# Token loads on two queues, conditioning in 1 MB halves and four places, tokens transposed first, eight leading projections

## The chip, the cores and the metric

One core of a Trainium2 chip runs the kernel. The metric is the time of one execution on the device in microseconds, as the median of several runs; a profile is one execution recorded instruction by instruction. The engines are the tensor engine (PE, with its weight loads as PEld), the vector engine (DVE), the scalar engine (ACT), GpSimd (POOL) and SyncE (SP), which here only issues DMAs. ACT and POOL issue DMAs too. Each engine works through its own queue in order.

## What is computed

A trunk of two layers over 128 context tokens and 512 latent tokens of width 2048, all in float32. The even layer (first) mixes windowed attention (A) with a gated short convolution (B), the odd layer differential attention (C) with dense attention (D). Both project the normalized and modulated tokens with one wide matrix, and both end in an output projection:

```python
def modulation(cond, w, b):
    m = jax.nn.silu(cond) @ w + b
    ...
    return jnp.split(m, 3, axis=-1)

    for layer in range(DEPTH):
        sh_p, sc_p, gt_p = modulation(c_ctx, ada_w[layer], ada_b[layer])
        sh_s, sc_s, gt_s = modulation(c, ada_w[layer], ada_b[layer])
        hp = rms_norm(xp, norm_g[layer]) * (1.0 + sc_p) + sh_p
        hs = rms_norm(xs, norm_g[layer]) * (1.0 + sc_s) + sh_s
        ...
        xp = xp + gt_p * out_p
        xs = xs + gt_s * out_s
```

`ada_w` is 2048 x 6144 per layer, 50 MB; its first two thirds (shift and scale) of layer 0 are needed before the first projection can be finished. The even layer's `ev_w_in` is 2048 x 6656: 52 projections of 128 columns.

## The kernel before

**Layout.** Features lie on the 128 partitions, tokens along the free axis: 640 columns, in two halves of 320 (`HV`). The inner dimension 2048 is 16 k tiles of 128. Every float32 operand is split into a high and a low part (`split`: ACT makes the high part, DVE the low one), and a product is three matmuls: high x high, high x low, low x high (lines 265 to 267). One projection is 16 k tiles x 2 halves x 3 = 96 of these.

**Start.** Ten token tiles `xb` (five blocks of 128 tokens, two tiles of 512 KB each) are loaded on ACT's queue (`x_load`, line 97), small rows (`rows_a`, `rows_b`: conditioning vectors, norms, biases) on SP's and POOL's. ACT computes `th`, a tanh of the conditioning rows (line 119), DVE finishes the SiLU (120), PE transposes the rows (123, 124). `x_block` then transposes each token block: 16 transposes in four groups of four (844), each group copied out of PSUM into `xT` by DVE or, the fourth, ACT (845); ACT also takes the squares for the RMS norm (849), and POOL the power of -0.5 (853). Two PSUM tiles `T` (`psT`) alternate there. `x_rows` spreads the norm over partitions (859, 860).

**Conditioning on PE.** `ada_on_pe` computes 256 or 512 columns of shift or scale: it loads `ada_w` in pieces of 2 MB into the tiles `ada_t`, of which there are two, multiplies them with the SiLU vectors (167), copies the result on ACT (170), transposes it (173), and DVE reduces it and adds bias and gain (175, 155, 144). `ada_group(g, js)` does scale and shift for k tiles js of group g (four groups of four).

**Leading projections.** While shift and scale still arrive, `run_tiles` goes over the k tiles in *units* and does the first projections side by side, so that each weight of the conditioning unlocks work at once. `cut` splits the first and last group of four k tiles into two units, so there are six: k tiles 0-1, 2-3, 4-7, 8-11, 12-13, 14-15. In each unit `h0_maker` makes the k tile's input (882, 886, 887; `h_t` has two tiles), and then every lead gets its matmuls. Two leads are *held*, in PSUM of their own, for the whole stage; the others (`trans`) share the PSUM pair `pa`/`pb` number 0, and after each unit their result is added to a sum in SBUF: by ACT in the first unit (332), by DVE afterwards (334). Weights `raw` come in by SP (243), four places for `raw`, four each for its halves `wh` and `wl`. After a unit's first lead, `ahead` issues the conditioning of the next unit.

**Behind the leads** the remaining projections run one after another; the leads' results are taken up one by one in between (`pending`, `prep`), and after `GRACE` projections what is left is finished at once (`settle`). Per projection and quarter, 1.2 steps of a filler run (`fill0`: the remaining conditioning on DVE, line 202, 12 blocks of 16 + 1 steps).

**What sets the order.** The text is not the order in the queues: a scheduler places the instructions of each engine when the program is built. DMAs of SP and ACT take their completion semaphores from a shared set of eight in turn (DMAHW0 to DMAHW7 below), and one that reuses a semaphore waits until the DMA that had it has landed.

## Time and profile before

| what | us |
|---|---|
| median of 3 runs | 2345.85 |
| lowest, highest | 2345.31, 2351.35 |
| span of the profiled execution | 2344.7 |
| PE busy | 2285.0 (97%) |
| PEld busy | 2207.7 (94%) |
| DVE busy | 1571.3 (67%) |
| ACT busy | 929.0 (40%) |

The span is that of the profiled execution from its first to its last instruction, and what lies around it is not in it; the runs' times are of whole executions. A matmul's record in the profile is longer than its share of the time, since matmuls overlap: the distance of two starts is the pace. An engine's idle time is put down to what released it ("<-").

### The profile page before, as it was taken

The page shows a single profiled execution, that of the slowest core. Times are in us where ns is not written, and L with a number is a line of the kernel's source. Part 1 is how long each engine was busy: PE and PEld are TensorE (multiplying, and loading weights), DVE is VectorE, ACT ScalarE, POOL GpSimd, SP SyncE. Part 2 cuts the span into 40 slices and gives each one's busy share as a digit, 9 for nine tenths or more (in the row PEclk, how much of TensorE's full clock was granted, in tenths as well). Part 3 has the DMA queues.
Part 4 walks back from the last instruction along what each step waited for, and adds up shares of the span by engine and source line. Part 5 has one row for each costly group of instructions (what it writes and reads, how often), then busy time and mean ns, then how long its engine had stood idle before and what let it go on. Part 6 is the DMA issues. An engine that isn't in the chain of part 4 may idle for free.

```text
span 2344.7 us, 41429 instructions
## 1 busy us (share of the span) xinstructions
PE 2285.0 (97%) x15988; PEld 2207.7 (94%) x15988; DVE 1571.3 (67%) x3196; ACT 929.0 (40%) x1935; POOL 133.0 (6%) x181
## 2 busy tenths in 40 slices
PE   4999999999999999999999999999999999999999
PEld 2689999999999999999999999999999999999999
DVE  3457977777777663888865755854855754567576
ACT  3234442442422222544553433434434444444343
POOL 1001000000000000000010100101000000000101
PEclk9999999999999999999999999999999999999999
DMA  7986535535355542954431421512423312128642
GB/s 241 334 268 188 160 107 166 161 91 179 113 173 170 166 137 82 291 158 132 160 100 57 130 87 57 151 57 84 138 67 92 106 50 77 46 74 272 181 121 69
DMA packets 390533, 321.94 MB, mean 137 GB/s; under 512 B 18306, under 2 KB 336272, under 8 KB 389824
## 3 DMA queue, kind: packets, MB, share of 16 engines
q1 hardware_dynamic: 381536, 285.83, 40.3%
q0 software_dynamic: 7216, 28.16, 3.3%
q10 hardware_dynamic: 1584, 5.31, 0.6%
q8 instruction: 125, 2.05, 0.3%
q14 instruction: 72, 0.59, 0.1%
HBM read 290.79 MB, written 28.44 MB: 136 GB/s over the span
## 4 chain that ended last, share of the span: by engine, by line
PE 52%; DVE 2%; DMA 1%; ACT 1%; issue 1%; POOL 0%; SPq 0%; POOLq 0%; DVEq 0%; ACTq 0%
PE pa L265 5%; PE pb L266 5%; PE pb L265 5%; PE pb L267 5%; PE pa L266 5%; PE pa L267 5%; PE pq L515 4%; PE pq L517 4%; PE pq L516 4%; PE T L693 1%; PE S L705 1%; PE S L707 1%; PE S L706 1%; PE T L544 1%; DMA yin<-yd 1%; PE T L754 1%
## 5 line engine op out<-in xcount | busy, mean ns | idle before, releaser
L230 ACT ACTIVATE wh<-raw 128x512 fp32r<-128x512 f32 (+1 forms) x490 | 303.6, 620 | 806.2 <-PE pb L266 671.4
L231 DVE TENSOR_TENSOR wl<-raw,wh 128x512 fp32r<-128x512 f32 (+1 forms) x490 | 331.2, 676 | 363.2 <-ACT wh L230 337.9
L265 PE MATMUL pa<-h,wh 128*128 128x320 f32 x1760 | 560.3, 319 | 1.8 <-ACT h L230 1.5
L266 PE MATMUL pa<-h,wh 128*128 128x320 f32 x1760 | 547.0, 311 | 1.4 <-DVE h L231 1.3
L267 PE MATMUL pa<-h,wl 128*128 128x320 f32 x1760 | 545.5, 310 | 0.0
L265 PE MATMUL pb<-h,wh 128*128 128x320 f32 x1760 | 545.2, 310 | 0.0
L267 PE MATMUL pb<-h,wl 128*128 128x320 f32 x1760 | 545.1, 310 | 0.0
L266 PE MATMUL pb<-h,wh 128*128 128x320 f32 x1760 | 544.4, 309 | 0.0
L202 DVE SCALAR_TENSOR_TENSOR acc<-adaw,sT,acc 128x512 f32<-128x512 f32 (+1 forms) x600 | 357.2, 639 | 10.3 <-DMA adaw<-in_ada_w 9.6
L265 PEld LDWEIGHTS pa<-h,wh 128*128 128x128 f32 x1760 | 331.4, 188 | 23.0 <-issue 16.4
L266 PEld LDWEIGHTS pa<-h,wh 128*128 128x128 f32 x1760 | 332.0, 189 | 6.5 <-issue 2.5
L267 PEld LDWEIGHTS pa<-h,wl 128*128 128x128 f32 x1760 | 331.4, 188 | 1.2 <-issue 1.2
L267 PEld LDWEIGHTS pb<-h,wl 128*128 128x128 f32 x1760 | 330.4, 188 | 2.1 <-issue 2.1
L265 PEld LDWEIGHTS pb<-h,wh 128*128 128x128 f32 x1760 | 330.3, 188 | 1.5 <-issue 0.8
L266 PEld LDWEIGHTS pb<-h,wh 128*128 128x128 f32 x1760 | 330.4, 188 | 0.1
L679 ACT ACTIVATE p<-S,nm,rq 128x768 f32<-128x768 f32 (+3 forms) x120 | 101.2, 844 | 114.7 <-DVE nm L674 83.3
L515 PE MATMUL pq<-h,wh 128*128 128x320 f32 x352 | 109.9, 312 | 0.8 <-ACT wh L230 0.8
L516 PE MATMUL pq<-h,wh 128*128 128x320 f32 x352 | 108.7, 309 | 0.0
L517 PE MATMUL pq<-h,wl 128*128 128x320 f32 x352 | 108.4, 309 | 0.0
L672 DVE TENSOR_REDUCE nm<-S 128x1 f32<-128x768 f32 (+3 forms) x120 | 91.9, 766 | 15.9 <-PE S L707 14.8
L230 ACT ACTIVATE pth<-T 128x512 fp32r<-128x512 f32 (+1 forms) x132 | 65.9, 533 | 71.4 <-PE T L693 71.3
L516 PE MATMUL pq<-T,wh 128*128 128x320 f32 x264 | 81.4, 308 | 0.0
(301 smaller groups left out, 3382.1 us busy)
## 6 DMA issues: line engine op xcount, KB each, us to landing
raw<-in_od_w_in SPq DMA_DIRECT2D x208, 256.0 KB, 2.8
raw<-in_ev_w_in SPq DMA_DIRECT2D x196, 256.0 KB, 2.9
adaw<-in_ada_w SPq DMA_DIRECT2D x192, 256.0 KB, 2.9
ada<-in_ada_w SPq DMA_DIRECT2D x16, 2048.0 KB, 9.1
adaw<-in_ada_w SPq DMA_DIRECT2D x128, 128.0 KB, 2.2
yd<-y POOLq DMA_DIRECT2D x34, 320.0 KB, 2.7
yin<-yd SPq DMA_DIRECT2D x32, 320.0 KB, 4.7
w<-yd SPq DMA_DIRECT2D x32, 320.0 KB, 4.3
```

Of the source, the lines that this page charges most:

```text
L202: V.scalar_tensor_tensor(out=a, in0=w, scalar=sT[:, kt, c:c + 1], in1=a, op0=ALU.mult, op1=ALU.add)
L230: A.activation(hi, x, AF.Copy)
L231: V.tensor_sub(lo, x, hi)
L265: PE.matmul(ps, wh[:, i, :], hi[:, sl], start=(j == js[0] if alone else (pos == 0 and j == 0)), stop=False)
L266: PE.matmul(ps, wh[:, i, :], lo[:, sl], start=False, stop=False)
L267: PE.matmul(ps, wl[:, i, :], hi[:, sl], start=False, stop=(j == js[1] - 1 if alone else (pos == 3 and j == 3)))
L515: PE.matmul(ps, wh[:, j, :], hi, start=(h == 0 and j == 0), stop=False)
L516: PE.matmul(ps, wh[:, j, :], lo, start=False, stop=False)
L517: PE.matmul(ps, wl[:, j, :], hi, start=False, stop=(h == 1 and j == 3))
L544: PE.transpose(t[:, i * P:(i + 1) * P], src(b), ident)
L672: V.tensor_reduce(nm, s, axis=AX.X, op=ALU.max, negate=True)
L679: A.activation(p[:, 0:n], s, AF.Exp, scale=rsc, bias=nm, accum_out=l)
```

## The change

- The token tiles of blocks 0 and 1 are still loaded on ACT's queue; those of blocks 2 to 4 are now loaded on SP's queue, ahead of the conditioning. Two of the small row loads go from SP to POOL.
- The conditioning tiles become four of 1 MB in place of two of 2 MB (same total), used in turn.
- All five token blocks are transposed ahead of the first conditioning; the first shift follows right behind, and no longer as `lead_in` of the leading stage.
- Eight leads in place of six: `TRANS` has six shared projections in place of four, and the list begins with u, c, k, v, g, q, q, g (it was u, k, v, g, q, q).
- Every group of k tiles is cut, so there are eight units of two k tiles, and their conditioning blocks are 256 columns wide throughout. `keep`, which writes the transposed tokens to DRAM once a unit is done, is tied to units 6 and 7 in place of 4 and 5.

```diff
@@ -40,7 +40,7 @@
 
 P_BUFS = 4
 W_BUFS = 4
-TRANS = [0, 3, 4, 5]
+TRANS = [0, 1, 4, 5, 6, 7]
 GRACE = 3
 RAW_AHEAD = 5
 SPLIT_AHEAD = 3
@@ -94,15 +94,15 @@
         ts = []
         for g in range(2):
             ts.append(hpool.tile([P, 1024], F32, tag=f"h{15 - 2 * b - g}", name="xb"))
-            nc.scalar.dma_start(ts[g], src[:, g * 1024:(g + 1) * 1024])
+            (nc.scalar if b < 2 else nc.sync).dma_start(ts[g], src[:, g * 1024:(g + 1) * 1024])
         return ts
 
 
     nc.sync.dma_start(rows_a[0:16, :], I["c"].rearrange("b (k p) -> (b k) p", p=P))
     nc.sync.dma_start(rows_a[16:32, :], I["c_ctx"].rearrange("(k p) -> k p", p=P))
     nc.sync.dma_start(ident, I["k_ident"])
-    nc.sync.dma_start(rows_a[32:64, :], I["norm_g"].rearrange("l (k p) -> (l k) p", p=P))
-    nc.sync.dma_start(rows_a[64:112, :], I["ada_b"][0].rearrange("(k p) -> k p", p=P))
+    nc.gpsimd.dma_start(rows_a[32:64, :], I["norm_g"].rearrange("l (k p) -> (l k) p", p=P))
+    nc.gpsimd.dma_start(rows_a[64:112, :], I["ada_b"][0].rearrange("(k p) -> k p", p=P))
     xs = [x_load(b) for b in range(5)]
     rows_b = wpool.tile([P, P], F32, tag="raw", name="rows_b")
     nc.gpsimd.dma_start(rows_b[0:48, :], I["ada_b"][1].rearrange("(k p) -> k p", p=P))
@@ -111,7 +111,7 @@
     for i, n in enumerate(("a_q_norm", "c_q_norm", "d_q_norm")):
         nc.gpsimd.dma_start(rows_b[74 + i:75 + i, :], I[n])
 
-    ada_t = [pre.tile([P, 4096], F32, name=f"ada{i}") for i in range(2)]
+    ada_t = [pre.tile([P, 2048], F32, name=f"ada{i}") for i in range(4)]
     ada_sb = pre.tile([P, 512], F32, name="ada_sb")
     h_t = [pre.tile([P, NT], F32, name=f"ht{i}") for i in range(2)]
 
@@ -156,11 +156,11 @@
 
     def ada_on_pe(l, cb, h=0, n=4):
 
-        acc, m, wd = psT(), 32 // n, n * P
+        acc, m, wd = psT(), 16 // n, n * P
         for kt in range(KT):
             if kt % m == 0:
                 w = ada_t[0].rearrange("p (k n) -> p k n", k=m)
-                ada_t.reverse()
+                ada_t.append(ada_t.pop(0))
                 nc.sync.dma_start(w, I["ada_w"][l, kt * P:(kt + m) * P, cb * 512 + h * 256:cb * 512 + h * 256 + wd]
                                   .rearrange("(k p) n -> p k n", p=P))
             g = kt % 4
@@ -310,7 +310,7 @@
         lead = len(leads)
         pps = {n: (sums[n][:, 0:HALF], sums[n][:, HALF:NT]) if n in trans
                else new_pp(1 + held.index(n) if trans else n) for n in leads}
-        units = [(pos, qd, js) for pos, qd in enumerate(order) for js in (cut if cut and pos in (0, 3) else [(0, 4)])]
+        units = [(pos, qd, js) for pos, qd in enumerate(order) for js in (cut or [(0, 4)])]
         for ui, (pos, qd, js) in enumerate(units):
             raws = {n: load_raw(w_ap, jobs[n][0], qd, js) for n in leads[:W_BUFS]}
             if ui == 0 and lead_in:
@@ -868,12 +868,12 @@
             nc.sync.dma_start(band, I["k_band"])
             load_rows(sink, "a_sink")
 
-    for b in range(4):
+    for b in range(5):
         x_block(b, xs[b])
     ada_on_pe(0, 4, 0, 2)
-    x_block(4, xs[4])
     x_rows((0, 1, 2, 3))
     x_rows((4,))
+    ada_on_pe(0, 0, 0, 2)
 
     def h0_maker(k):
         x = xT[k // 4][:, k % 4, :]
@@ -892,7 +892,7 @@
 
 
     def keep(ui, n, pp):
-        g = {(4, 0): 0, (4, 4): 1, (5, 0): 2, (5, 4): 3}.get((ui, n))
+        g = {(6, 0): 0, (6, 4): 1, (7, 0): 2, (7, 4): 3}.get((ui, n))
         if g is not None:
             V.tensor_copy(xTm[g][:, 4 * NT:], pp[1][:, 0:1])
             nc.gpsimd.dma_start(x0dram[g], xTm[g])
@@ -1014,9 +1014,9 @@
         b_tiles(i)
 
     u0, c0, b0, h0, g0, g1 = jobs[4:10]
-    jobs[0:10] = [u0, jobs[0], jobs[1], g0, jobs[2], jobs[3], g1, c0, b0, h0]
+    jobs[0:10] = [u0, c0, jobs[0], jobs[1], g0, jobs[2], jobs[3], g1, b0, h0]
     run_tiles(jobs, I["ev_w_in"][0], h0_maker, fill0, FILL0, ada_group, trans=TRANS, grace=GRACE, cut=((0, 2), (2, 4)),
-              summed=keep, led=even_start, lead_in=lambda: ada_on_pe(0, 0, 0, 2))
+              summed=keep, led=even_start)
     drain(prep)
     for _ in fill0:
         pass
```

What the scheduler made of it, at three places. First ACT's queue from its beginning (`xb` are token tiles, `wh<-raw` a weight split, `sqj` the squares of a token tile). Before, from the third load on:

```order
L97 DMA xb<-in_x_sample 128x1024 [waits DMAHW0_49]
L97 DMA xb<-in_x_sample 128x1024 [waits DMAHW1_49]
L97 DMA xb<-in_x_sample 128x1024 [waits DMAHW2_49]
L97 DMA xb<-in_x_sample 128x1024 [waits DMAHW3_49]
L97 DMA xb<-in_x_sample 128x1024 [waits DMAHW5_49]
L97 DMA xb<-in_x_sample 128x1024 [waits DMAHW6_49]
L97 DMA xb<-in_x_prompt 128x1024 [waits DMAHW7_49]
L97 DMA xb<-in_x_prompt 128x1024 [waits DMAHW0_49]
L119 ACT_TABLE_LOAD
L119 ACTIVATE th<-rows_a 32x128
L849 ACTIVATE sqj,s_189<-xb 128x1024
L230 ACTIVATE wh<-raw 128x256 [waits DMAHW3_49]
```

Now:

```order
L97 DMA xb<-in_x_sample 128x1024 x3
L97 DMA xb<-in_x_sample 128x1024 [waits DMAHW1_49]
L119 ACT_TABLE_LOAD
L119 ACTIVATE th<-rows_a 32x128 [waits DMAHW2_49]
L849 ACTIVATE sqj,s_191<-xb 128x1024 [waits DMAHW0_49]
L849 ACTIVATE sqj,s_191<-xb 128x1024 [waits DMAHW5_49,Activation_49]
```

Six loads have left the queue ahead of `th`; the four weight splits that stood between the squares stand behind all token blocks now.

Second, PE's queue from its beginning, as the difference of the two (`T<-ident,xb` are token transposes, `T<-ada,sT` conditioning, `T<-ident,rx` the norm's spreading):

```order
 L123 MATMUL T<-ident,rows_a 128x112
 L124 MATMUL T<-ident,rows_b 128x77
-L844 MATMUL T<-ident,xb 128x128 x64
-L167 MATMUL T<-ada_120,sT 32x256 x16
+L844 MATMUL T<-ident,xb 128x128 x80
+L167 MATMUL T<-ada_120,sT 32x256 x8
+L167 MATMUL T<-ada_121,sT 32x256 x8
 L173 MATMUL T<-ident,ada_sb 128x128 x2
-L844 MATMUL T<-ident,xb 128x128 x16
 L859 MATMUL T<-ident,rx 128x128 x5
-L167 MATMUL T<-ada_121,sT 32x256 x16
+L167 MATMUL T<-ada_122,sT 32x256 x8
+L167 MATMUL T<-ada_123,sT 32x256 x8
```

The fifth token block has moved ahead of the first conditioning, and each conditioning block now reads two tiles.

Third, SP's queue in the leading stage of the change, about one unit (`raw` are weights of the leads, each of 128 KB; `ada` tiles of conditioning, each of 1 MB):

```order
L164 DMA ada_120<-in_ada_w 128x8x256 [waits DMAHW5_49,PE_49]
L243 DMA raw<-in_ev_w_in 128x2x128 [waits DMAHW6_49,DMAHW1_49,DVE_49]
L243 DMA raw<-in_ev_w_in 128x2x128 [waits DMAHW7_49,DMAHW2_49,DVE_49]
L243 DMA raw<-in_ev_w_in 128x2x128 [waits DMAHW3_49,DMAHW0_49,DVE_49]
L243 DMA raw<-in_ev_w_in 128x2x128 [waits DMAHW4_49,DVE_49]
L164 DMA ada_121<-in_ada_w 128x8x256 [waits PE_49]
L164 DMA ada_122<-in_ada_w 128x8x256 [waits PE_49]
L164 DMA ada_123<-in_ada_w 128x8x256 [waits PE_49]
```

Of the four conditioning tiles of a unit, one stands ahead of four weight loads and three behind them; each weight load waits for DVE to have split an earlier one.

## The prediction

> **What bounds the kernel now.** I read the page first: PE is busy for 97% of the span, so only time in which PE has nothing to do, or computes below its pace, can be won. Its 40 slices show such time in the first slice alone. I then cut the first 300 us with the view of windows: up to PE's first instruction, up to the first projection matmul, the six leading projections (with their last quarter again by itself), and a stretch behind them.
>
> ```profile
> core 0: us, PE busy (x) PEld busy (x) DVE busy (x) ACT busy (x) POOL busy (x), PEclk, DMA share, GB/s
> 0.00:24.30 24.30, 0.00 (x0) 0.00 (x0) 0.87 (x4) 1.92 (x3) 3.37 (x10) 1.00 0.93 331
> 24.30:56.50 32.20, 22.02 (x170) 14.84 (x170) 15.65 (x43) 16.90 (x35) 2.78 (x5) 1.00 0.52 164
> 56.50:182.30 125.80, 121.66 (x916) 96.55 (x917) 67.83 (x164) 39.19 (x84) 1.92 (x4) 0.99 0.89 304
> 150.00:182.30 32.30, 32.27 (x257) 29.68 (x256) 19.42 (x50) 8.53 (x19) 1.92 (x4) 1.00 0.68 231
> 215.00:290.00 75.00, 74.80 (x543) 70.70 (x542) 72.19 (x157) 37.31 (x84) 5.02 (x6) 1.00 0.49 146
> ```
>
> PE does nothing for 24.3 us; then 32.2 us of token work go by in which DMA runs at half its share. In the leading stage PE is the fullest engine and DMA the second (0.89). From 215 to 290 us DVE is full: 72.19 of 75. Why PE starts so late stands in the timelines of ACT and PE:
>
> ```profile
> 0.75 8.59 ACTq L97 DMA_DIRECT2D xb<-in_x_sample  x8
> 21.52 0.82 ACTq L97 DMA_DIRECT2D xb<-in_x_prompt  x2
> 22.37 1.28 ACT L119 ACT_TABLE_LOAD   x1 [22.37 <-DMA ada<-in_ada_w]
> 23.66 0.31 ACT L119 ACTIVATE th<-rows_a 32x128 f32<-32x128 f32 x1
> 30.58 0.42 ACT L230 ACTIVATE wh<-raw 128x256 fp32r<-128x256 f32 x1 [5.57 <-DMA raw<-in_ev_w_in]
> ```
>
> ```profile
> 24.34 0.45 PE L123 MATMUL T<-ident,rows_a 112*128 112x112 f32 x1 [24.34 <-DVE rows_a L120]
> 32.11 1.11 PE L844 MATMUL T<-ident,xb 128*128 128x128 f32 x4 [5.30 <-DVE xT L845]
> 34.48 4.42 PE L844 MATMUL T<-ident,xb 128*128 128x128 f32 x20 [1.26 <-DVE xT L845]
> 44.90 1.93 PE L167 MATMUL T<-ada,sT 128*32 128x256 f32 x32 [0.19 <-DVE xT L845]
> 47.60 1.09 PE L844 MATMUL T<-ident,xb 128*128 128x128 f32 x8
> 49.03 1.25 PE L844 MATMUL T<-ident,xb 128*128 128x128 f32 x8 [0.34 <-DVE xT L845]
> 50.56 1.35 PE L859 MATMUL T<-ident,rx 128*128 128x128 f32 x10 [0.28 <-DVE xT L845]
> 56.50 0.41 PE L265 MATMUL pa<-h,wh 128*128 128x320 f32 x1 [0.24 <-ACT h L886]
> ```
>
> ACT issues eight token loads by 9.3 us and then stands until 21.5: the ninth reuses a semaphore that the first 2 MB conditioning load (ada) still holds. So `th` comes at 23.66 and PE's first instruction right behind it. Soon ACT waits again, 5.57 us for a weight block whose split stands between the token squares; DVE, in order, waits with it, and PE for DVE (5.30 us).
>
> **The start, part by part.** ACT now issues four token loads and SP six, before SP's first ada load; the only semaphore ACT still waits for was used by a small load ahead. `th` can then run once its rows are in and the table load of 1.28 us is done, by about 8 us (estimated: half of the issues that took until 9.3, then the table load, and 2 us to spare). What is late next is POOL's queue: PE's first two instructions need `rows_a` and `rows_b`, and POOL now has eight small loads instead of six.
>
> ```profile
> L112 POOL DMA_DIRECT2D rows_b<-in_d_q_norm x1: 484/484/484, 4.0 to 4.0; - x1
> DMA to landing us min/median/max: 5.8/6.0/6.3
> 2.11 0.66 SPq L104 DMA_DIRECT2D rows_a<-in_norm_g  x1
> 2.82 0.55 SPq L105 DMA_DIRECT2D rows_a<-in_ada_b  x1
> ```
>
> The last of the six was issued at 4.0 us and landings took at most 6.3; the two moved loads cost 0.66 + 0.55 us on SP. I take the same on POOL: 4.0 + 1.2 + 6.3 = 11.5 us for PE's start. The ten tokens are 5.24 MB; at 331 GB/s they are all in after 15.8 us, so the first blocks are there at 11.5 and the last ones before their turn.
>
> A token block is 16 transposes in four groups, with their copies on DVE and ACT. The fifth block, run when no weight split stood in it, took from 47.60 to 50.56, 2.96 us; the groups behind 34.48 went at 4.42/5 = 0.88 us each, 3.5 us per block, at the array's slower pace. Five blocks take 14.8 to 17.7 us; I take 16, so they end at 27.5 us. Behind them comes the first ada block (44.90 to 47.60 before, 2.7 us) and then what stood before from 50.56 to 56.50, 5.9 us. Its four weight splits are now behind the blocks on ACT and DVE; tokens, 4.2 MB of ada and 0.5 MB of weights are 10 MB, in by 30 us at 331 GB/s, while ACT is ready for them at about 29. The first projection matmul stands at 27.5 + 2.7 + 5.9 = 36.1 us, bounds 34.5 and 39: **20.4 us earlier**.
>
> **The leading stage.** Counted from 56.50, 576 projection matmuls (L265 to L267) had started when the one at 182.07 came, and 768 at 215.05. Two more projections are the 192 between. Their pitch, and what stood in their way:
>
> ```profile
> 70.63 0.31 PE L266 MATMUL pa<-h,wh 128*128 128x320 f32 x1
> 72.98 0.31 PE L267 MATMUL pa<-h,wl 128*128 128x320 f32 x1
> 182.07 0.37 PE L265 MATMUL pa<-h,wh 128*128 128x320 f32 x1
> 215.05 0.31 PE L265 MATMUL pa<-h,wh 128*128 128x320 f32 x1
> 84.06 1.92 PE L167 MATMUL T<-ada,sT 128*32 128x512 f32 x16
> 90.03 3.36 PE L167 MATMUL T<-ada,sT 128*32 128x512 f32 x16 [4.05 <-DMA ada<-in_ada_w]
> 84.00:93.30 9.30, 5.25 (x33) 1.01 (x32) 2.56 (x6) 2.02 (x4) 0.00 (x0) 0.82 1.08 383
> ```
>
> Sixteen steps in 2.35 us are 0.147 each, so 192 are 28.2 us. That is moved work, not added work: it goes from behind the stage into it. What can go away is the wait at 86 us, 4.05 us for an ada load, and the slow block behind it (3.36 us for work that took 1.92; the granted clock of that stretch is 0.82): 5.4 us. It arose in the two units that ran uncut, where 8 MB of ada were due at once through two 2 MB places. Now all eight units are alike. One has on PE 96 matmuls (14.1 us), two ada blocks (3.9) and their four small transposes: some 18.4 us. It loads 4.2 MB of ada and 1 MB of weights; at the 304 GB/s of this stage that takes 17 us, at the 383 above 13.6. PE stays the bound, narrowly.
>
> ```profile
> L334 DVE TENSOR_TENSOR sum<-sum,pa 128x320 f32<-128x320 f32 x20 | 9.7, 485 | 12.0 <-PE pa L267 11.5
> L231 DVE TENSOR_TENSOR wl<-raw,wh 128x256 fp32r<-128x256 f32 x20 | 8.3, 421 | 15.7 <-ACT wh L230 15.7
> L887 DVE SCALAR_TENSOR_TENSOR h<-ht,mod,h 128x512 fp32r<-128x512 f32 x16 | 12.0, 749 | 3.3 <-ACT h L886 3.3
> L887 DVE SCALAR_TENSOR_TENSOR h<-ht,mod,h 128x128 fp32r<-128x128 f32 x16 | 5.5, 347 | 0.0
> ```
>
> Added on DVE: L334 runs 84 times instead of 40, 44 x 0.485 = 21 us, and 40 small weight splits (421 ns) stand for 20 large ones. One unit asks of DVE twelve sums (5.8 us), eight splits (3.4), two k tiles through L882 and L887 (4 x (0.75 + 0.35) = 4.4) and about one us for the shift and scale: 14.6 of 18.4, 79%. The cut units of before asked 8 sums, six splits and the same rest, 11.8 us a unit, and in the two such units at the stage's end, which the stretch from 150 to 182.3 holds, PE was busy for 32.27 of 32.30 us. So the sums lie under matmuls; if that cover went, the price is the rival below. For new stalls in the stage I allow 0 to 10 us (up to 1.5 at each of seven unit ends) and take 2.
>
> **Behind it.** DVE is full there, and the same DVE work now has two projections less of PE work over it.
>
> ```profile
> L202 DVE SCALAR_TENSOR_TENSOR acc<-adaw,sT,acc 128x512 f32<-128x512 f32 x42 | 30.2, 744 | 0.0
> L231 DVE TENSOR_TENSOR wl<-raw,wh 128x512 fp32r<-128x512 f32 x17 | 11.6, 685 | 0.0
> ```
>
> Two projections fewer take 28.2 us of PE away from that place, and of DVE's work what is tied to their slots: 2 x 4 x 1.2 filler steps of two L202 (14.3 us) and 8 splits (5.5), 19.8 us. Where DVE sets the pace, 28.2 - 19.8 = 8.4 us come back as PE waits; where PE still leads, none. At 96% against PE's near 100% it lies between: I take 4. The filler's 204 steps (12 blocks of 17) fit the 44 x 4 x 1.2 = 211 slots that are left.
>
> **Sum** against the profiled span of 2344.7 us: -20.4 (start) - 5.4 (wait and slow block) + 2 + 4 = -19.8, so a span of 2324.9. The median of the runs is 2345.85, 1.2 above that span; 2345.85 - 19.8 = **2326 us**. With all terms at their good bounds (22 + 5.4) it is 2318, at their bad ones (17.5 + 5.4 - 10 - 8.4 = 4.5) 2341.
>
> **Rivals.** *Conditioning behind the weights (slower).* On SP three of a unit's four ada loads stand behind four weight loads, which wait for DVE to split the four before them, in turn waiting for weight places that PE frees half a unit in, about 9 us. 3.1 MB then land 8 to 10 us later, at the next unit's start; they are needed 3 to 9 us into it. If each of seven unit ends pays the 5.4 us of the one above, that is 37.8 instead of 5.4: 2345.85 - 20.4 + 37.8 - 5.4 + 4 = 2362. It turns slower than before once a unit end costs over 3.1 us. For it: the DMA share of 0.89, and ACT and DVE waiting for weight blocks in this stage. Against: those waits did not reach PE before. Chance 0.08.
>
> *Sums in a row.* The leads outside the held two share one PSUM pair, and four follow each other in each unit now, where two did. If each such step waits for one L334 (0.485 us), 32 steps cost 15.5 us instead of the 2 I allow: 2339.5. Against it stands the stretch from 150 to 182.3. Chance 0.10.
>
> *The start gains less.* POOL's loads now compete with token loads on a full DMA (0.93 before 24.3 us); if they take twice their 6.3 us, PE starts at 17.8, and if the array stays at its slow pace through all five blocks (17.7 us), the first projection is at 44: 8 us of the gain gone, 2334. The Trainium skill ("TensorE: Matmul & The Clock Gate", What's actually happening) says that the array starts at half clock and needs some 3.4 us of sustained work to leave it. By that rule short bursts between token copies could keep it slow. Here transposes ran at 0.22 us until 38 us and at half that behind, so the trace bears the rule out, and shows that 4 us of closely set transposes were enough. Chance 0.14.
>
> **How the numbers follow.** The forecast has 0.68 with an own range of 2318 to 2336. A measurement of this kernel can tell 0.3%, 7 us. Faster: 0.67 of the forecast, 0.13 of the weaker start, 0.03 of the sums, 0.83. Within 7 us: 0.06 of the sums and 0.03 of the others, 0.09. Slower: 0.08. The range 2316 to 2341 leaves the slower rival out and little else.
>
> **What would show it.** `th` near 8 us, PE's first instruction at 11 to 13, the first L265 at 34 to 39, token blocks without a weight split between them. The 768th projection matmul near 187 us instead of 215.05. L167 with no wait for ada above 1 us, the clock at 1.00 throughout the stage. In the stretch behind, DVE above 95% with more PE idle than 0.2 of 75 us. Wrong it would be if L167 waits at each unit's start, or if L265 behind L334 shows gaps of half a microsecond.

## The result and the profile after

The changed kernel takes 2330.23 us (median of 4 runs, 2327.19 to 2331.45). The kernel before, run beside it on the same chip, takes 2348.6 (2345.31 to 2352.28): ratio 0.9915, 95% interval 0.9902 to 0.9928, so 18.4 us or 0.8% faster. The forecast was 2326, with a range of 2316 to 2341.

The profiled execution of the changed kernel has a span of 2329.7 us (2344.7 before). The view of windows, cut at PE's first instruction, at the first projection matmul and at the 768th, and the stretch behind the leads as in the prediction:

```profile
core 0: us, PE busy (x) PEld busy (x) DVE busy (x) ACT busy (x) POOL busy (x), PEclk, DMA share, GB/s
0.00:7.79 7.79, 0.00 (x0) 0.03 (x1) 0.87 (x4) 3.78 (x6) 4.37 (x12) 1.00 0.73 239
7.79:36.64 28.85, 21.09 (x170) 14.03 (x170) 15.90 (x42) 15.57 (x32) 2.78 (x5) 1.00 1.05 361
36.64:187.33 150.69, 149.29 (x1235) 128.56 (x1235) 96.86 (x246) 49.28 (x121) 2.19 (x4) 1.00 0.87 282
215.00:290.00 75.00, 74.90 (x538) 68.48 (x537) 66.99 (x150) 45.94 (x104) 8.26 (x7) 1.00 0.38 112
```

The start is 20 us shorter, and the same token work now runs with DMA at a share of 1.05 where it had 0.52. In the leading stage PE is busy for 149.29 of 150.69 us at a clock of 1.00. Behind it DVE is less full than before (66.99 of 75, then 72.19).

ACT's and PE's timelines from the beginning show what replaced the wait at the ninth load:

```profile
0.75 2.38 ACTq L97 DMA_DIRECT2D xb<-in_x_sample  x4
3.15 1.28 ACT L119 ACT_TABLE_LOAD   x1 [3.15 <-DMA rows_a<-in_c]
5.26 0.31 ACT L119 ACTIVATE th<-rows_a 32x128 f32<-32x128 f32 x1 [0.82 <-DMA rows_a<-in_c_ctx]
```

```profile
7.79 0.42 PE L123 MATMUL T<-ident,rows_a 112*128 112x112 f32 x1 [7.79 <-DMA rows_a<-in_ada_b]
12.03 0.36 PE L124 MATMUL T<-ident,rows_b 77*128 77x77 f32 x1 [3.82 <-DMA rows_b<-in_d_q_norm]
12.19 5.25 PE L844 MATMUL T<-ident,xb 128*128 128x128 f32 x24
17.79 1.25 PE L844 MATMUL T<-ident,xb 128*128 128x128 f32 x8 [0.35 <-DVE xT L845]
26.42 1.25 PE L844 MATMUL T<-ident,xb 128*128 128x128 f32 x8 [0.29 <-DVE xT L845]
27.86 1.93 PE L167 MATMUL T<-ada,sT 128*32 128x256 f32 x32 [0.19 <-DVE xT L845]
35.69 1.02 PE L167 MATMUL T<-ada,sT 128*32 128x256 f32 x10 [0.47 <-DMA ada<-in_ada_w]
36.64 0.41 PE L265 MATMUL pa<-h,wh 128*128 128x320 f32 x1
152.14 0.38 PE L265 MATMUL pa<-h,wh 128*128 128x320 f32 x1 [1.32 <-DVE sum L334]
187.33 0.39 PE L265 MATMUL pa<-h,wh 128*128 128x320 f32 x1
```

`th` comes at 5.26 us in place of 23.66. PE's second instruction waits for the last small row (POOL's queue), as the prediction had it, and the token blocks then run without a weight in between: 20 transposes at the slow pace (0.21 us and more from start to start, until 16.84 us), the later ones at 1.14 to 1.26 us for eight. What PE still waits for after the start (the view of waits, from 36 to 300 us: total, times, longest):

```profile
PE T L544 <- DVE m L589: 2.8, 1, 2.8
PE pa L265 <- DVE sum L334: 1.3, 1, 1.3
PE T L167 <- DMA ada<-in_ada_w: 0.5, 1, 0.5
```

Set side by side by the number of projection matmuls that have started, the change leads by 19.86 us at the first, 27.72 at the 768th (where two projections more have been led), 20.79 at the 1344th, 19.75 at the 2000th (445.2 us before) and 17.97 at the 6400th. This lead, "the gain at matmul n", is used below. At the last projection matmul of the two profiles it is 14.7. I take these last 3.3 us for spread: all the kernels of this document lose something behind the 6400th matmul against the same profile of before. Seven of them have there, behind a pause of PE near 1340 us, a stretch of 3.4 us at half the granted clock, which the profile of before has not; these lose 3.63 to 6.41 us, and the other six, the changed kernel among them, 0.57 to 3.55. The profile of before also comes from one of the faster executions of its kernel: its span is 2344.7 us, and the 58 on record with a span reach from 2341.4 to 2354.3, with a median of 2347.75.

### The profile page after: what moved, and what is told of

The parts are those of the page before. It is cut to its first block, busy times and chain, and to the rows that moved or that the text cites. A ratio compares the mean times of both kernels' runs of the same rounds, so it can differ in the third digit from the quotient of the medians.

```text
span 2329.7 us, 41919 instructions
## 1 busy us (share of the span) xinstructions
PE 2287.0 (98%) x16116; PEld 2213.1 (95%) x16116; DVE 1595.3 (68%) x3270; ACT 934.5 (40%) x1963; POOL 134.6 (6%) x183
## 4 chain that ended last, share of the span: by engine, by line
PE 87%; DVE 5%; DMA 4%; ACT 2%; issue 1%; POOL 1%; SPq 0%; POOLq 0%; DVEq 0%; ACTq 0%
PE pa L265 10%; PE pb L266 10%; PE pb L265 10%; PE pb L267 10%; PE pa L266 10%; PE pa L267 10%; PE pq L515 4%; PE pq L517 4%; PE pq L516 4%; PE T L693 2%; PE S L705 2%; PE S L707 1%; PE S L706 1%; DMA yin<-yd 1%; PE T L167 1%
## 5 line engine op out<-in xcount | busy, mean ns | idle before, releaser
L265 PE MATMUL pa<-h,wh 128*128 128x320 f32 x1760 | 561.9, 319 | 3.2 <-ACT h L230 1.6
L265 PE MATMUL pb<-h,wh 128*128 128x320 f32 x1760 | 544.7, 310 | 0.0
L202 DVE SCALAR_TENSOR_TENSOR acc<-adaw,sT,acc 128x512 f32<-128x512 f32 (+1 forms) x600 | 356.5, 637 | 23.3 <-DMA adaw<-in_ada_w 22.0
L265 PEld LDWEIGHTS pa<-h,wh 128*128 128x128 f32 x1760 | 331.9, 189 | 23.8 <-issue 17.0
L265 PEld LDWEIGHTS pb<-h,wh 128*128 128x128 f32 x1760 | 330.5, 188 | 0.7 <-issue 0.4
L231 DVE TENSOR_TENSOR ptl<-T,pth 128x512 fp32r<-128x512 f32 (+1 forms) x132 | 77.7, 608 | 6.7 <-ACT pth L230 5.4
```

The source lines that it names most:

```text
L202: V.scalar_tensor_tensor(out=a, in0=w, scalar=sT[:, kt, c:c + 1], in1=a, op0=ALU.mult, op1=ALU.add)
L231: V.tensor_sub(lo, x, hi)
L265: PE.matmul(ps, wh[:, i, :], hi[:, sl], start=(j == js[0] if alone else (pos == 0 and j == 0)), stop=False)
```

## The experiments

In the table "first" is the start of the first projection matmul L265, "gain" that at the 2000th matmul in the profiles; each ratio is to the runs of the kernel before that were made beside it.

| kernel | median us | ratio, interval | first | gain |
|---|---|---|---|---|
| changed kernel | 2330.23 | 0.9915, 0.9902 to 0.9928 | 36.6 | 19.75 |
| e3_queues_only | 2332.51 | 0.9931, 0.9916 to 0.9947 | 36.8 | 17.25 |
| e1_start_only | 2330.38 | 0.9918, 0.9900 to 0.9937 | 36.6 | 19.57 |
| e6_acts_queue | 2345.18 | 0.9985, 0.9976 to 0.9995 | 55.1 | 3.80 |
| e10_prompt_on_pool | 2344.25 | 0.9983, 0.9973 to 0.9992 | 52.7 | 3.60 |
| e9_rows_late | 2334.22 | 0.9939, 0.9924 to 0.9954 | 35.4 | 17.07 |
| e2_leads_only | 2343.46 | 0.9973, 0.9962 to 0.9984 | 55.3 | 7.09 |
| e7_halves_only | 2345.62 | 0.9986, 0.9976 to 0.9997 | 55.6 | 3.35 |
| e8_six_leads_cut | 2338.28 | 0.9961, 0.9946 to 0.9976 | 36.5 | 8.51 |
| e13_eight_old_cut | 2335.30 | 0.9933, 0.9921 to 0.9946 | 36.5 | 17.26 |
| e5_two_2mb | 2330.09 | 0.9918, 0.9904 to 0.9931 | 36.0 | 22.41 |
| e11_fill_later | 2329.72 | 0.9923, 0.9910 to 0.9937 | 36.6 | 23.92 |
| e15_2mb_fill | 2329.64 | 0.9907, 0.9888 to 0.9925 | 36.0 | 24.01 |

### Which part makes the start

**e1_start_only**: the kernel before with the new queues, the 1 MB tiles and the new order of the tokens; six leads and the old cuts stay. It is the diff of the change without these lines, and without the order of `jobs` and the units of `keep` that go with them:

```diff
-TRANS = [0, 3, 4, 5]
+TRANS = [0, 1, 4, 5, 6, 7]
-... for js in (cut if cut and pos in (0, 3) else [(0, 4)])]
+... for js in (cut or [(0, 4)])]
```

> Before with the queue edit, the 1 MB halves and the token order, but six leads and their cut as before. Theory (the gain is the earlier start: ACT no longer stands behind the conditioning load's semaphore, and weight splits leave the token blocks): first projection matmul at 36 to 38 us, time 17 to 21 us below before. Rival (eight leads give PE work while conditioning arrives; an earlier start is eaten by waits for conditioning): first projection as early, but 4 us or more of new waits for ada in the stage and a gain of 10 us or less.

Measured: ratio 0.9918 beside the changed kernel's 0.9915, and a gain that stays at 19.6 from the 672nd matmul to the 4000th; the theory holds. The start with its queues, halves and token order gives as much as the whole change.

**e3_queues_only**: the queues alone.

```diff
-            nc.scalar.dma_start(ts[g], src[:, g * 1024:(g + 1) * 1024])
+            (nc.scalar if b < 2 else nc.sync).dma_start(ts[g], src[:, g * 1024:(g + 1) * 1024])
-    nc.sync.dma_start(rows_a[32:64, :], I["norm_g"]...
-    nc.sync.dma_start(rows_a[64:112, :], I["ada_b"]...
+    nc.gpsimd.dma_start(rows_a[32:64, :], I["norm_g"]...
+    nc.gpsimd.dma_start(rows_a[64:112, :], I["ada_b"]...
```

> Before with the token loads on two queues and the two row loads on POOL, nothing else. Theory (the queue edit alone makes the start): th near 5 us, PE's first instruction near 12, first projection matmul at 37 to 41 us, time 14 to 20 us below before. Rival (token order and halves are needed too): a new wait ahead of the first conditioning keeps the first projection behind 46 us, and the gain is under 9 us.

Measured: ratio 0.9931, first L265 at 36.8, gain 17.25; the theory holds. Three edited lines make the start. In ACT's timeline the first weight splits now run in one row, behind the first four token blocks:

```profile
25.55 1.34 ACT L230 ACTIVATE wh<-raw 128x256 fp32r<-128x256 f32 x4
```

The wait for conditioning remains, 4.69 us, and the block behind it is slow again (3.26 us), as in the kernel before:

```profile
66.37 1.92 PE L167 MATMUL T<-ada,sT 128*32 128x512 f32 x16
72.98 3.26 PE L167 MATMUL T<-ada,sT 128*32 128x512 f32 x16 [4.69 <-DMA ada<-in_ada_w]
```

In e1, with halves, that wait is 1.3 us. The step from e3 to e1 (halves and token order together) is 2.3 us in gain and 2.1 in the medians; their intervals overlap, so the runs alone don't show it.

**e6_acts_queue**: the changed kernel with the token and row loads back on their old queues (the inverse of the diff above).

> The changed kernel with its token and row loads put back on ACT's and SP's queues as before. Theory: the ninth token load waits for an earlier DMA again, weight splits stand between the token blocks, the first projection matmul is at 46 us or later, and the time is 4 to 10 us below before instead of about 18. Rival (token order, halves and leads make the gain): first projection before 42 us, 13 us or more below before.

Measured: ratio 0.9985, 4.4 us faster by the medians, first L265 at 55.1, gain 3.8; the theory holds, at its near edge. ACT's timeline has its wait back, and at 30.43 us a weight split between the token squares, which waits 5.95 us for its `raw`:

```profile
0.74 10.99 ACTq L97 DMA_DIRECT2D xb<-in_x_sample  x8
13.04 8.77 ACTq L97 DMA_DIRECT2D xb<-in_x_prompt  x2
21.85 1.28 ACT L119 ACT_TABLE_LOAD   x1 [21.85 <-DMA ada<-in_ada_w]
```

Smaller conditioning loads release the semaphore of the ninth load earlier (13.04 us in place of 21.5), and then the tenth waits until 21.8. With loads half as large the stand ends at the same time, one load later.

**e10_prompt_on_pool**: the kernel before with only the ninth and tenth load moved, to POOL's queue. The queue edit removes two things at once, ACT's stand at the ninth load and the weight splits between the token squares; this kernel removes the first alone.

```diff
-            nc.scalar.dma_start(ts[g], src[:, g * 1024:(g + 1) * 1024])
+            (nc.scalar if b < 4 else nc.gpsimd).dma_start(ts[g], src[:, g * 1024:(g + 1) * 1024])
```

> The kernel before with only the two x_prompt loads (the ninth and tenth of ACT's queue) on POOL's queue. It tells apart two reasons for the gain of the start: that ACT stood at the ninth load until a semaphore came free, and that the weight splits between the token squares made ACT and DVE wait for weights. Theory A (the ninth load's wait is the main cost): th at 10 to 12 us, PE starts at 11 to 13 us, first L265 at 38 to 42 us, time 12 to 17 us below before, ratio 0.993 to 0.995. Theory B (splits between the squares hold the tokens until the first weights land, at about 28 us): PE starts at 11 to 13 us but the token blocks wait for DVE behind wl, first L265 at 45 to 54 us, time 2 to 10 us below before.

Measured: theory B. ACT, DVE and PE in their timelines:

```profile
11.30 0.31 ACT L119 ACTIVATE th<-rows_a 32x128 f32<-32x128 f32 x1
29.82 0.42 ACT L230 ACTIVATE wh<-raw 128x256 fp32r<-128x256 f32 x1 [14.80 <-DMA raw<-in_ev_w_in]
```

```profile
30.27 0.43 DVE L231 TENSOR_TENSOR wl<-raw,wh 128x256 fp32r<-128x256 f32 x1 [13.65 <-ACT wh L230]
```

```profile
12.92 4.40 PE L844 MATMUL T<-ident,xb 128*128 128x128 f32 x20
31.79 6.26 PE L844 MATMUL T<-ident,xb 128*128 128x128 f32 x28 [14.47 <-ACT xT L845]
```

`th` is there at 11.3 and PE begins on tokens at 12.92, as in the changed kernel. But a weight split is next on ACT, and its `raw` lands at 29.8 us, where it landed before the edit too (30.58). All three engines stand for 14 us, and of the 12 us won at PE's start 3.8 are left at the first projection. So the free semaphore alone is worth 3.8 us of the 19.7 that the queue edit wins at the first projection (e3); the rest comes only when the order of work on ACT and DVE changes too, with no weight split between token blocks. What the order alone would win was not measured. Behind ACT's stand, the profile of before has 5.30 and 1.26 us in which PE waits between token groups, so I estimate 6 to 7 us: less than the rest. The two waits lie over each other, and each hides most of the other.

**e9_rows_late**: the changed kernel with the transposes of `rows_a` and `rows_b` behind the third token block, so that the tokens need not wait for POOL's small loads.

```diff
+    def rows_in():
         t0 = psT()
         PE.transpose(t0[:, 0:112], rows_a[0:112, :], ident[0:112, 0:112])
         PE.transpose(t0[:, 128:205], rows_b[0:77, :], ident[0:77, 0:77])
...
         x_block(b, xs[b])
+        if b == 2:
+            rows_in()
```

> The changed kernel with PE's transposes of rows_a and rows_b moved behind the third token block, so that the first token transposes no longer stand behind POOL's eight small loads. Theory (PE's start is set by the last small row load, 12.0 us in the changed kernel): PE starts at 5 to 8 us, the first L265 stands at 30 to 34 us in place of 36.6, the time is 2 to 6 us below the changed kernel, ratio to before 0.989 to 0.991. Rival (behind the rows, the DMA engines at a share of 0.98 set the first 36 us): PE starts earlier but waits for xb, ada or raw, first L265 at 35 us or later, no change in time. Rival (transposes spread out thinly by the arrival of the tokens stay at half clock for all blocks): token blocks at 3.5 us each, first L265 at 35 us or later.

Measured: ratio 0.9939, gain 17.07, so no gain and rather a loss of 2.7 us. The third possibility happened, for three of the five blocks. PE starts at 6.66, and goes at the slow pace until past 19 us (the added lines move L844 to L846 here):

```profile
6.66 4.88 PE L846 MATMUL T<-ident,xb 128*128 128x128 f32 x20 [6.66 <-DMA ident<-in_k_ident]
12.32 1.11 PE L846 MATMUL T<-ident,xb 128*128 128x128 f32 x4 [0.79 <-DVE xT L847]
14.22 5.59 PE L846 MATMUL T<-ident,xb 128*128 128x128 f32 x24 [0.78 <-DVE xT L847]
20.49 3.54 PE L846 MATMUL T<-ident,xb 128*128 128x128 f32 x20
24.38 1.10 PE L846 MATMUL T<-ident,xb 128*128 128x128 f32 x8 [0.34 <-ACT xT L847]
```

There are two breaks of 0.8 us, in which PE waits for the copies of earlier tokens, and the array stays slow beyond them: the first 46 transposes take 0.21 us and more each, until 19.4 us, and most of the later ones 0.11. The last block ends at 26.5 us in place of 27.9, and the first projection is 1.2 us earlier. These are lost again at once: from 36 to 41 us the granted clock is 0.66 (it is 0.50 from 36.6 to 40.0),

```profile
36.00:41.00 5.00, 5.00 (x29) 3.03 (x27) 1.33 (x4) 1.41 (x4) 0.00 (x0) 0.66 1.09 349
```

and the wait for a sum at 151 us grows to 3.4 us, with another stretch at half clock behind it (0.51 from 156.0 to 159.4). The Trainium skill ("TensorE: Matmul & The Clock Gate", What's actually happening) has the array leave half clock after a busy window of about 3.4 us, and says that this window runs freely, so that the moment varies with where the work falls in it. By that rule a run of close transposes needs between one and two such windows, 3.4 to 6.8 us (an estimate from that figure). The traces agree: the pace changed after 3.7 us in e10, 3.9 before (from 34.48 us), 4.7 in the changed kernel, 5.3 in e9 (from 14.22) and 5.6 in e10's second run (from 31.79), while e9's first run of 4.5 us was not enough.

### What the leading stage is worth

**e2_leads_only**: the kernel before with eight leads and every group cut (the order of `jobs` and the units of `keep` go with them); the start stays.

```diff
-TRANS = [0, 3, 4, 5]
+TRANS = [0, 1, 4, 5, 6, 7]
-... for js in (cut if cut and pos in (0, 3) else [(0, 4)])]
+... for js in (cut or [(0, 4)])]
```

> Before with eight leads, all units cut, and nothing else. Theory: first projection matmul at 56 to 58 us as before; the 4 us wait for ada and the half-clock block are gone (about -5), some 3 us come back behind the stage: time between 6 us below and 2 us above before. Rival (the leads bring the gain): 10 us or more below before.

Measured: ratio 0.9973, 6 us faster, at the far edge of the theory, and the first projection at 55.3, a little before its 56. The gain is 12.8 us at the 768th matmul and 7.1 at the 2000th: the wait for conditioning is gone, and 5.7 us are given back behind the stage.

**e7_halves_only**: the kernel before with four tiles of 1 MB.

```diff
-    ada_t = [pre.tile([P, 4096], F32, name=f"ada{i}") for i in range(2)]
+    ada_t = [pre.tile([P, 2048], F32, name=f"ada{i}") for i in range(4)]
-        acc, m, wd = psT(), 32 // n, n * P
+        acc, m, wd = psT(), 16 // n, n * P
-                ada_t.reverse()
+                ada_t.append(ada_t.pop(0))
```

> The kernel before with its conditioning tiles as four of 1 MB, nothing else changed. Theory (the halves and the eight leads remove the same wait, and neither touches the start): first L265 stays at 56 to 57 us, the wait for ada that PE had at 86 us (4.05 us in the kernel before) falls below 2 us; the time is 2 to 6 us below before, ratio 0.997 to 0.999. Rival (the halves do nothing by themselves; the wait comes from how much conditioning the uncut units ask for at once): the wait stays above 3.5 us and the time is within 2 us of before. Rival (more and smaller loads cost the queue): slower than before by over 3 us.

Measured: ratio 0.9986, 3 us faster by the medians; the theory holds. PE's longest wait for ada in the stage is 1.5 us, the gain 3.35. So halves alone and leads with cuts alone both remove the same wait, and cannot be added up.

**e5_two_2mb**: the changed kernel with two tiles of 2 MB (the diff above turned round).

> The changed kernel with its conditioning tiles as two of 2 MB again; queues, order of the tokens, eight leads and eight cut units stay. Theory (with eight leads in cut units a conditioning block is loaded a whole unit ahead, so that the halves are no longer needed there): at most 3 us slower than the changed kernel, ratio 0.991 to 0.994, waits of L167 for ada below 3 us in all. Rival (two places are too few once every unit is cut): each unit start waits 1 us or more for ada, and the time is 5 us or more above the changed kernel.

Measured: ratio 0.9918, median 2330.09; the theory holds. Once all units are cut and have eight leads, the halves do nothing for the time; the profile even has 2.7 us more gain, with no wait of 1 us or more for the sum at 151 us.

**e8_six_leads_cut**: the changed kernel with six leads.

```diff
-TRANS = [0, 1, 4, 5, 6, 7]
+TRANS = [0, 3, 4, 5]
-    jobs[0:10] = [u0, c0, jobs[0], jobs[1], g0, jobs[2], jobs[3], g1, b0, h0]
+    jobs[0:10] = [u0, jobs[0], jobs[1], g0, jobs[2], jobs[3], g1, c0, b0, h0]
```

> The changed kernel with six leads in the old order of jobs in place of eight; its start, its 1 MB tiles and its eight cut units stay. Theory (on top of the start and the halves the two more leads add nothing): within 3 us of the changed kernel, ratio to before 0.991 to 0.993, first L265 at 36 to 37 us, no wait of L167 for ada above 3 us although each unit has four matmul runs fewer to hide its loads. Rival (the leads are needed to cover 1 MB loads in cut units): waits of L167 for ada at several unit starts, together over 5 us, and a time of 2335 or more.

Measured: ratio 0.9961, gain 8.51: 11 us worse than both the changed kernel and e1. The theory falls, and the rival's time fits, but not its mechanism: L167 never waits for ada. Ahead of its last units PE shows hardly any idle time, and yet it is slow. Its timeline in one unit of e8, and in one of the changed kernel:

```profile
70.14 0.31 PE L265 MATMUL pb<-h,wh 128*128 128x320 f32 x1
70.37 0.62 PE L167 MATMUL T<-ada,sT 128*32 128x256 f32 x2
70.92 0.42 PE L266 MATMUL pa<-h,wh 128*128 128x320 f32 x1
71.18 0.31 PE L267 MATMUL pa<-h,wl 128*128 128x320 f32 x1
71.41 0.64 PE L167 MATMUL T<-ada,sT 128*32 128x256 f32 x8
71.98 0.42 PE L266 MATMUL pb<-h,wh 128*128 128x320 f32 x1
```

```profile
78.06 0.31 PE L267 MATMUL pb<-h,wl 128*128 128x320 f32 x1
78.30 1.93 PE L167 MATMUL T<-ada,sT 128*32 128x256 f32 x30
80.16 0.41 PE L265 MATMUL pa<-h,wh 128*128 128x320 f32 x1
80.41 0.31 PE L266 MATMUL pa<-h,wh 128*128 128x320 f32 x1
```

Between projections the starts are 0.147 us apart. From the last projection matmul ahead of a conditioning piece to the first one behind it, almost a whole block of 32 takes 2.10 us (78.06 to 80.16), and a piece of only two or eight matmuls 0.8 (70.14 to 70.92). Some 0.37 us of each piece do not depend on its size: they are the price of going over and back (the working is in the last section). In e8 the scheduler put conditioning in more and smaller pieces: up to the 1344th projection matmul PE goes from a conditioning matmul to a projection 38 times in e8, 21 times in the changed kernel, 16 in e5 and 25 in e1, which differs from e8 in the cut alone. From the last projection matmul ahead of each piece to the first behind it, without idle time, these stretches add up to 41.4 us in e8, 34.0 in the changed kernel, 32.0 in e5 and 36.7 in e1. So the smaller pieces are 4.7 of the 11.1 us that e8 loses on e1 by that matmul, and 7.4 of the 12.3 that it loses on the changed kernel. The rest comes from the last units, where PE runs out of work twice (view of waits of e8):

```profile
PE pa L265 <- DVE sum L334: 3.0, 1, 3.0
PE pa L265 <- ACT wh L230: 1.8, 1, 1.8
```

In all, PE is idle 2.3 us longer than in e1 up to there. And behind each of the two waits the granted clock is 0.5 for 3.4 us (from 153.2 and from 173.7): projection matmuls then start 0.266 us apart in place of 0.147, which costs 3.2 us together. The three sums are 10.2 of the 11.1 us.

**e13_eight_old_cut**: the fourth corner, the changed kernel with eight leads and only the first and last group cut.

```diff
-... for js in (cut or [(0, 4)])]
+... for js in (cut if cut and pos in (0, 3) else [(0, 4)])]
-        g = {(6, 0): 0, (6, 4): 1, (7, 0): 2, (7, 4): 3}.get((ui, n))
+        g = {(4, 0): 0, (4, 4): 1, (5, 0): 2, (5, 4): 3}.get((ui, n))
```

> The changed kernel with the old rule of cuts: eight leads in six units (only the first and the last group of k tiles are cut), the fourth corner beside six leads in six units (the start alone, ratio 0.9918), six leads in eight units (0.9961) and eight in eight (the changed kernel). Theory (cutting every group costs about 10 us, because it puts conditioning between the projections in more and smaller pieces, and two more leads pay it back, because a unit then has more matmuls to cover its loads and the pieces lie further apart): with eight leads and no such cost the time is 3 to 8 us below the changed kernel, ratio to before 0.988 to 0.990, and PE goes from a conditioning matmul to a projection matmul fewer times than the 21 of the changed kernel. Rival (cuts cost only where the loads set the pace; with eight leads they set it no more, whatever the cut): within 3 us of the changed kernel, ratio 0.991 to 0.993. Rival (the uncut units ask for 4 MB of conditioning twice as far apart and PE waits for it): waits of L167 for ada over 3 us, slower than the changed kernel by 3 us or more.

Measured: ratio 0.9933, gain 17.26, and 24 of these transitions, not fewer than 21. The theory falls, and neither rival fits: the median is 5 us above the changed kernel's, which the second rival has, but the waits for ada come to 2.0 us, below its 3, and the intervals overlap. At the 1344th matmul the four corners have gained

| | old cuts | all groups cut |
|---|---|---|
| six leads | 19.57 (e1) | 8.51 (e8) |
| eight leads | 19.51 (e13) | 20.79 (changed kernel) |

The leads are worth nothing with the old cuts. Cutting every group costs 11 us with six leads and nothing with eight. The two edits belong together, and together give 1.2 us here and 0.2 at the 2000th matmul, where eight leads with the old cuts are 2.3 us behind six (table above). Only the step to e8 is clear in the runs too.

### What is given back behind the stage

**e11_fill_later**: the changed kernel with the filler on DVE (L202) starting four projections later.

```diff
-FILL0 = 1.2
+FILL0 = 1.3
-              summed=keep, led=even_start)
+              summed=keep, led=even_start, fill_from=16)
```

> The changed kernel in which the filler on DVE (L202) begins four projections later and then goes a little faster (1.3 steps a quarter in place of 1.2); the work is the same. Theory (the part of the gain that is given back behind the leading stage is paid to a crowded DVE): the wait of PE at L544 for DVE (2.97 us at 205 us) falls below 1.5 us, the gain at the 2000th projection matmul rises from 19.75 to 21 to 23 us, the time is 1 to 4 us below the changed kernel, ratio 0.990 to 0.992. Rival (the filler is not what DVE is late with there; the leads' results are): the wait stays above 2 us and the time does not change.

Measured: PE's wait at L544, 2.8 us in the changed kernel's view of waits (the expectation's 2.97 is the distance of two starts less the pace), is now

```profile
PE T L544 <- DVE m L589: 1.3, 1, 1.3
```

and the gain at the 2000th matmul is 23.92, more than the theory asked for. So DVE's crowding does hold up the first results behind the leads. The shorter wait is 1.5 of the 4.2 us won. In the changed kernel a stretch of 3.4 us at half the granted clock follows it (0.50 from 208.0 to 211.4), in which matmuls start 0.266 us apart; e11 has no such stretch there, which is about as much again. And up to the 2000th projection matmul e11 has done ten matmuls fewer for the filler's results (L208 and L214). The median is 2329.72 against 2330.23, runs from 2325.19 to 2334.98: the time of a whole execution does not show it. Part of it is given back soon, when e11 has done those too: its gain is 20.90 at the 4000th matmul.

**e15_2mb_fill**: e5 and e11 together.

> The two pieces that gained in the profile, together: the changed kernel with two conditioning tiles of 2 MB and with the later filler. Theory (the two act at different places, the one at the last units' sums and the switches between conditioning and projections, the other at L544 behind the stage): the wait at 151 us (1.49 us in the changed kernel) stays away, the wait at L544 is below 1.5 us, the gain at the 2000th projection matmul is 24 to 27 us (19.75 in the changed kernel, 22.4 and 23.9 with each alone), and the time is 2 to 7 us below the changed kernel, ratio to before 0.988 to 0.991. Rival (what is won up to 450 us is lost in the spread of the later layer): the gain at the 2000th matmul is there in the profile, but the median of the runs lies within 2 us of the changed kernel.

Measured: gain 24.01 at the 2000th matmul, 21.4 at the 4000th, 16.6 at the end; median 2329.64, ratio 0.9907. The waits at 151 us and at L544 are as the theory has them, and the time is as the rival has it, within 2 us of the changed kernel. Its ratio is the lowest of all, but its interval covers the changed kernel's 0.9915; that it is faster than the changed kernel is not shown.

## Why the prediction was right

**The start** was forecast as 20.4 us and measured as 19.86. `th` comes at 5.26 us (about 8 was forecast), and PE's tokens, which wait for the last small row, begin at 12.19 us (forecast 11.5); the blocks end at 27.86 (27.5), the first projection is at 36.64 (36.1). The slow pace lasted 4.7 us and the five blocks 15.7, where 16 was taken. Of the two causes that the prediction named, it gave the semaphore first, and it did not say what each is worth alone. e10 shows that the semaphore alone is worth little: with it free and the weight split in place 3.8 us are won, with both gone 19.7 (e3). The forecast holds because the edit removes both.

**The leading stage** was forecast at 5.4 us saved and 2 paid. At equal work, 182.07 + 28.2 = 210.3 stands against 187.33, so 23.0 us earlier; less the start's 19.9 these are 3.1 saved, for 3.4 forecast. The wait for conditioning is gone (0.5 us once, at the start), and the clock is 1.00. The price paid is one wait for a sum, at 152.14. The rival of the sums in a row shows in that place alone. The rival of conditioning behind the weights didn't happen: no unit start waits for ada. What the prediction didn't have is what e8 and e13 show: that cutting every group has a price of its own, of 11 us with six leads, which the two more leads keep away. It took PE's work per unit as a sum of matmuls and left out the transitions between the two kinds (4.7 of these 11 us) and what a pause costs behind its end (3.2). And the saving in this stage doesn't need the leads: e1, with the start and the halves alone, has 19.57 us at the 2000th matmul, where the changed kernel has 19.75. That the two more leads keep away a price that the prediction had no term for is luck as far as its sum goes.

**Behind it** 4 us were to come back; 23.0 less 19.75 is 3.3, and e11 confirms that DVE's crowding is part of it. But PE waits there only 1.4 us longer than before (3.9 in place of 2.5 up to the 2000th matmul); the half clock behind the first wait, which the prediction did not have, costs about as much. The sign for it was wrong: DVE was to be above 95% busy from 215 to 290 us, and is at 89%. PE's longest wait, of 2.8 us at L544, comes at 205 us, ahead of that window. A share over 75 us did not show it; the list of waits did.

**The sum** was 19.8 us, and the gain at the 2000th matmul is 19.75. The medians differ by 18.4. The forecast time was 4.2 us low. Of these, 2.75 are the starting point, 2345.85 where the median beside the changed kernel is 2348.6; the other 1.4 are the difference of 19.8 and 18.4.

Executions of one kernel differ by up to 13 us (2343.15 to 2356.1), and the granted clock that is on record for each goes with it: of 58 executions of the kernel before, the four with the highest mean (0.999) took 2343.15 to 2345.31 us, the two with the lowest (0.994) 2355.31 and 2356.1. The profiles show one place. PE has the same pause of 1.44 or 1.45 us in all fourteen, at L1216 (L1220 in e9) between 1127 and 1149 us; the clock then is 0.5 for 6.8 us in six of them, for 3.4 in six, and not at all in e3 and e11. What decides this stays open. There are no two profiles of one kernel, so that the last 3.3 us of the profiles are spread is argued, not shown.

## What to carry to other kernels

When one engine's queue holds loads, small computations and work that depends on later loads, look for the first instruction in it that waits for something not needed yet: moving only what stood first (the ninth load) left the next such wait (a weight split) in its place, and only the edit that moved both paid. Cutting work into smaller units so that loads arrive in time can be paid in transitions on the engine that must alternate; count them, because they don't show as idle time. Where the tensor engine pauses, look at the granted clock behind the pause too: it can cost as much again. And a part that gains a few microseconds in one profiled execution is not faster until the runs say so, where they spread over ten.

## What the hardware showed that was not expected

- A conditioning matmul, 128 x 32 with 256 columns, set between projection matmuls, 128 x 128, costs far more than its share: 0.8 us for two or eight of them, 1.24 for 16, 2.10 for 32. Up to four of them start within 0.02 us of each other, and the next row of up to four 0.22 us later. The two matmuls came in two such rows, as the eight did. From 16 to 32 matmuls four more rows cost 0.86 us; less 0.215 for each row (2, 4 and 8 of them), some 0.37 of each piece do not depend on its size (an estimate), and PE counts as busy all the while. The Trainium skill ("TensorEngine Tiling (Array Packing)", Key Properties) says that changing the tiling mode drains the engine, without a price; these rows agree with it and give one.
- Starting PE's tokens 5.5 us earlier (e9) bought 1.2 us at the first projection: with breaks of 0.8 us between token groups the array stayed slow for 13 us.
- A pause can cost more than itself. In these fourteen profiles PE has eight pauses of 3.04 to 4.69 us behind the first projection, and at the end of each the granted clock is 0.5 for 3.4 us. Of pauses between 1.4 and 3.0 us some were followed by such a stretch (2.81 us in the changed kernel, 1.82 in e8) and some not (2.98 at 1339 us in the changed kernel, 2.32 in e13).
- A load of 1 MB in place of 2 MB ahead of a shared semaphore moved the wait from the ninth load to the tenth, and ACT was free at 21.85 us in place of 22.37.
